# A fifth gate block pair by seven products, with the forms' sums on GpSimd

## The chip, the cores and the metric

One core of one Trainium2 chip runs the whole program. The metric is the device time of one execution in microseconds (us); the median of three runs before the change is 2079.75 us (2079.65 to 2079.78). A profile is one further execution, with its own time.

## What is computed

A trunk of two layers over 512 tokens of width 2048, in f32. Layer 0 mixes by indexed sparse attention, layer 1 by stick-breaking attention against a shared K/V. After each mixer comes the piece that the change touches:

```python
x = _layer_norm(DN_ALPHA * x + y, ln_g[i], ln_b[i])
x = x + (p[i] @ w_ple[i]) * jax.nn.sigmoid(x @ w_ple_gate[i])
```

Here `x` is 512 x 2048 and `w_ple_gate[i]` 2048 x 2048. The program keeps `x` transposed, as 16 tiles of 128 rows (features) by 512 columns (tokens).

## The kernel before

**Products in three parts.** Every f32 operand is split into a high part (fp32r) and the rest: ScalarE (ACT) makes the high part, VectorE (DVE) subtracts it (`split`, L101 to L107, for activations; `split_w`, L293 to L304, for weights, `wh` on L302 and `wl` on L303). A product is then three matmuls on TensorE (PE): high by high, high by low, low by high. In a row of the trace the operands of L121 are `wh` with `h`, of L122 `wh` with `l`, of L123 `wl` with `h`.

**Chunks.** All weight work is a list of chunks, each with a 512 KB load into one of 6 `raw` buffers, a split into one of 3 `wh`/`wl` buffers, and its matmuls. `plan` (L309) fixes once, relative to the place of a chunk in the list, when its load, its split and its additions are written; there are no costs or priorities. Each engine then takes its instructions strictly in that written order, and each waits for its own inputs and buffers; so an engine runs ahead of the place in the list as far as its inputs allow.

**A plain block pair** (`block`) makes two output tiles of 128 features in 4 chunks of 24 matmuls, 128x512 each: 96 matmuls. **A pair by seven products** (`quads`, L194) cuts the 2 x 2 block problem (two output tiles by two token halves) Strassen fashion into the products P1 to P7, each 24 matmuls of 128x256: 168 matmuls. It needs sums of weight rows (two 512 KB loads that GpSimd issues as accumulating DMAs, L286, and two DVE additions, L291) and sums of the activations, the *forms* S1 to S4.

**The gate stage of a layer** (`gate_block`) comes behind the product with `w_ple` (`ple_chunks`, which also takes part of the layer norm between its chunks). Before the change, blocks 0 to 3 (output tiles 0 to 7) are plain and pairs 4 to 7 (tiles 8 to 15) go by seven products. Blocks 0 and 1 are zipped: chunks c0 and c1 run as one over feature tiles 0 to 3, c2 and c3 over tiles 4 to 7, c4 and c5 over 8 to 11, c6 and c7 over 12 to 15. Blocks 2 and 3 are c8 to c15. While c0 to c5 run, the layer norm of the 16 tiles is finished by `ln_tiles`: for each tile DVE subtracts the mean (L944) and multiplies by the inverse deviation (L945), ACT applies gain and bias (L953; for tiles 0 and 1 it is DVE, L951) and casts the high part (L955), and DVE subtracts for the low part (L959), tile by tile, with the weights' `wl` (L303) between.

**The forms of the gate stage** are made by `g_sums(layer, j)` for feature tiles 2j and 2j+1, from the normed tiles `dT`: four additions over halves and rows of 256 columns (L783 to L786), then a split (`split`, L105 and L106). Eight such calls are hung on chunks c8 to c14, all on DVE but for the split's cast. `u_more` makes S1 and S4 during the first two seven-product pairs. Results of the `w_ple` product are kept on chip for tiles 0 to 7 and stored and loaded again for tiles 8 to 15 (`pl_store`, L989; `pl_load`, L993).

`k.tt` takes one of 78 tile buffers of 128x512; `k.soon` and `chunk.then` hang a call behind a chunk.

Of the kernel before, what the change touches and what calls it, by code (L numbers as in the profile page):

```python
# [6 lines left out]
F32 = mybir.dt.float32  # L7
F32R = mybir.dt.float32r
I32 = mybir.dt.int32
AF = mybir.ActivationFunctionType  # L10
OP = mybir.AluOpType

P = 128
T = 512
NT = T // P
D = 2048
KT = D // P
# [14 lines left out]
HALF = T // 2  # L32
# [362 lines left out]
def _emit(k, xt, pt, positions, lncols, freq, w_in, w_out, w_gate, w_ple, w_kv, w_v, w_q, out):  # L395
    nc, const = k.nc, k.const
# [185 lines left out]
    u = {}  # L582
# [181 lines left out]
    uhl, u23, u14 = {}, {}, {}  # L764
# [13 lines left out]
    def g_sums(layer, j):  # L778

        a, b = dT[2 * j], dT[2 * j + 1]  # L780
        s, t = k.tt(s="s23"), k.tt(s="s14")
        lo, hi = slice(0, HALF), slice(HALF, T)
        nc.vector.tensor_tensor(t[:, hi], b[:, hi], a[:, hi], op=OP.subtract)  # L783
        nc.vector.tensor_tensor(s[:, hi], a[:, lo], a[:, hi], op=OP.subtract)
        nc.vector.scalar_tensor_tensor(s[:, lo], t[:, hi], -1.0, a[:, lo], op0=OP.mult, op1=OP.subtract)
        nc.vector.scalar_tensor_tensor(t[:, lo], s[:, lo], -1.0, b[:, lo], op0=OP.mult, op1=OP.subtract)  # L786
        u23[j], u[2 * j + 1] = k.split(s), [t, None]
        for m in (2 * j, 2 * j + 1):
            uhl[m] = xn[m]
            if m < 8:  # L790
                dt_done(layer, m)

    once = set()

    def dt_done(layer, m):

        if (layer, m) in once:
            dT[m] = None
        once.add((layer, m))
# [13 lines left out]
    def more_forms(qs, more):  # L813
        for n, name in enumerate(("P1", "P7", "P6", "P2")):
            qs[0][name].then(lambda n=n: more("S1", (2 * n, 2 * n + 1)))
        for q, name, js in ((0, "P4", (0, 1, 2)), (0, "P5", (3, 4, 5)), (1, "P7", (6, 7))):
            qs[q][name].then(lambda js=js: more("S4", js))
# [14 lines left out]
    def u_drop(what):  # L832
        for j in range(KT // 2):
            if what == 0:
                u23.pop(j)
            else:
                uhl.pop(2 * j + (what == 1))
                if what == 2:
                    u14.pop(j)
# [65 lines left out]

    def ln_rstd():
        r, var, q = ln["rstd"], ln.pop("var"), ln.pop("q")
        nc.scalar.activation(r, var, AF.Ln)
        nc.scalar.activation(r, r, AF.Exp, scale=-0.5)
        nc.vector.tensor_tensor(q, r, r, op=OP.mult)  # L910
        nc.vector.tensor_tensor(q, q, var, op=OP.mult)
        nc.vector.tensor_scalar(q, q, -0.5, 1.5, op0=OP.mult, op1=OP.add)
        nc.vector.tensor_tensor(r, r, q, op=OP.mult)
# [29 lines left out]
    def ln_norm(m):  # L943
        nc.vector.tensor_tensor(dT[m], dT[m], ln["mean"], op=OP.subtract)  # L944
        nc.vector.tensor_tensor(dT[m], dT[m], ln["rstd"], op=OP.mult)  # L945
# [15 lines left out]
    def ln_tiles(layer, lo, hi):  # L961

        for m in range(lo, hi):
            ln_high(layer, m)
            if m + 1 < KT:
                ln_norm(m + 1)
            ln_low(m)

    def ple_done(layer, m, ps):
        t = k.tt(s="ple")  # L970
        nc.scalar.copy(t, ps)
        pl[m] = t
        if m >= 8:
            k.soon(lambda: pl_store(layer, m))
        if m == 3:
            add_squares(nc.vector)
        elif m == 5:
            ln_stats()
        elif m == 7:
            ln_rstd()  # L980
            ln_norm(0)
        elif m in (12, 14):
            ln_tiles(layer, m // 2 - 6, m // 2 - 5)
# [3 lines left out]
    def pl_store(layer, m):  # L987
        pd[m] = k.dram.tile([P, T], F32, tag=f"pl{layer}_{m}", name=k.name("pld"))
        nc.sync.dma_start(pd[m], pl.pop(m))  # L989

    def pl_load(m):
        pl[m] = k.tt(s="ple")
        nc.sync.dma_start(pl[m], pd[m])  # L993
# [55 lines left out]
    def halves(m):  # L1049
        return (slice(256, 512), slice(0, 256)) if m == KT - 1 else (slice(0, T),)  # L1050

    def gate_block(layer, fin):
        def done(b, i, ps):
            m = 2 * b + i
            sg = k.tt(s="sg")
            for c in halves(m):
                nc.scalar.activation(sg[:, c], ps[:, c], AF.Sigmoid)
                nc.vector.tensor_tensor(sg[:, c], sg[:, c], pl[m][:, c], op=OP.mult)
                nc.vector.tensor_tensor(sg[:, c], sg[:, c], dT[m][:, c], op=OP.add)
            pl[m] = None  # L1060
            dt_done(layer, m)
            fin(m, sg)

        for b in range(4):
            k.block(w_gate[layer], 4 * b, lambda m: xn[m],
                    lambda i, ps, b=b: done(b, i, ps), pops=1)
            if b == 1:
                k.zip_last()
                for ch in k.chunks[-8:]:
                    ch.mms.sort(key=lambda m: m[0])  # L1070
                k.merge_last(8)
                k.chunks[-8].after = lambda: ln_tiles(layer, 5, 8)
                for n in range(4):
                    k.chunks[n - 7].after = lambda n=n: ln_tiles(layer, 2 * n + 8, 2 * n + 10)

        for n, js in enumerate(((0,), (1,), (2,), (3,), (4,), (5,), (6, 7))):
            k.chunks[n - 8].then(lambda js=js: [g_sums(layer, j) for j in js])
        k.chunks[-1].then(xn.clear)

        def done7(n, which, t):  # L1080
            m = 2 * n + 8 + which
            for c in halves(m):
                nc.scalar.activation(t[:, c], t[:, c], AF.Sigmoid, scale=-1.0 if which else 1.0)
                nc.vector.tensor_tensor(t[:, c], t[:, c], pl[m][:, c], op=OP.mult)
                nc.vector.tensor_tensor(t[:, c], t[:, c], dT[m][:, c], op=OP.add)
            pl[m] = dT[m] = None
            fin(m, t)

        qs = k.quads([((w_gate[layer], 2 * b), (w_gate[layer], 2 * b + 1)) for b in range(4, KT // 2)], u_form, done7)
        more_forms(qs, u_more)  # L1090
        for n, q in enumerate(qs):
            q["P7"].then(lambda n=n: pl_load(2 * n + 8))
            q["P4"].then(lambda n=n: pl_load(2 * n + 9))
        last = qs[-1]
        last["P6"].then(lambda: u_drop(0))
        last["P4"].then(lambda: u_drop(1))
        last["P3"].then(lambda: u_drop(2))
        return last
# [111 lines left out]
    qs = k.quads([(where_b[a](ha), where_b[b](hb)) for a, ha, b, hb in plan_b], form, b_done)  # L1210
# [43 lines left out]
def _pairs(w, pairs):  # L1254

    v = w.reshape(4, 4, P, -1)
    v = np.stack([np.concatenate([v[..., a:a + P], v[..., b:b + P]], -1) for a, b in pairs])
    return v.transpose(0, 1, 3, 2, 4).reshape(-1, P, 1024)
# [54 lines left out]
```

## Time and profile before

| | before |
|---|---|
| median of three runs | 2079.75 us |
| profiled execution: its time | 2079.5 us |
| profiled execution: span of the core | 2077.8 us |
| TensorE busy | 2066.6 us, 99% of the span, 13600 matmuls |
| VectorE busy | 1578.0 us, 76% |
| ScalarE busy | 1078.9 us, 52% |
| GpSimd busy | 259.1 us, 12% |

Busy time is a sum over a span with very different stages. Matmuls overlap in the pipeline, so the duration of one (some 0.28 us for 256 columns) is more than the pace at which they follow each other; the pace is read from start to start. A row of the windows view gives the stretch, its length, the busy time of PE, PEld (weight loads), DVE, ACT and POOL with their instructions, the granted clock, the DMA share and GB/s. A timeline row gives start, duration, engine, line, operation and tiles; a pair of brackets at its end says how long the engine sat idle before it and for whom.

### The profile page before, as it was taken

The page shows a single profiled execution, that of the slowest core. Times are in us where ns is not written, and L with a number is a line of the kernel's source. Part 1 is how long each engine was busy: PE and PEld are TensorE (multiplying, and loading weights), DVE is VectorE, ACT ScalarE, POOL GpSimd, SP SyncE. Part 2 cuts the span into 40 slices and gives each one's busy share as a digit, 9 for nine tenths or more (in the row PEclk, how much of TensorE's full clock was granted, in tenths as well). Part 3 has the DMA queues.
Part 4 walks back from the last instruction along what each step waited for, and adds up shares of the span by engine and source line. Part 5 has one row for each costly group of instructions (what it writes and reads, how often), then busy time and mean ns, then how long its engine had stood idle before and what let it go on. Part 6 is the DMA issues. An engine that isn't in the chain of part 4 may idle for free.

```text
span 2077.8 us, 34434 instructions
## 1 busy us (share of the span) xinstructions
PE 2066.6 (99%) x13600; PEld 1900.9 (91%) x13600; DVE 1578.0 (76%) x2434; ACT 1078.9 (52%) x1749; POOL 259.1 (12%) x325
## 2 busy tenths in 40 slices
PE   9999999999999999999999999999999999999999
PEld 7987888888888998899899999999999998998898
DVE  5576976565568899787877777777777778899786
ACT  4564345455554547455555545554455554556554
POOL 5201000000000120000011111111111110121000
PEclk9999999999999999999999999999999999999999
DMA  6322322222223664457454554555555563764464
GB/s 249 102 97 76 102 92 82 70 73 71 82 88 97 189 189 148 141 163 234 132 129 130 153 162 128 134 151 151 140 149 158 136 203 112 198 178 153 132 178 127
DMA packets 89298, 284.60 MB, mean 137 GB/s; under 512 B 10160, under 2 KB 10416, under 8 KB 89136
## 3 DMA queue, kind: packets, MB, share of 16 engines
q1 hardware_dynamic: 74736, 229.97, 32.0%
q0 software_dynamic: 14400, 52.44, 14.7%
q8 instruction: 106, 1.74, 0.3%
q14 instruction: 56, 0.46, 0.1%
HBM read 266.11 MB, written 16.25 MB: 136 GB/s over the span
## 4 chain that ended last, share of the span: by engine, by line
PE 89%; DVE 4%; issue 3%; ACT 2%; DMA 1%; SPq 0%; POOL 0%; DVEq 0%; POOLq 0%; ACTq 0%
PE g L187 43%; PE g L121 13%; PE g L123 13%; PE g L122 13%; PE s L592 2%; DVE wl L303 1%; PE o L122 1%; PE o L123 1%; PE o L121 1%; PE s L121 1%; PE s L122 1%; PE s L123 1%; ACT wh L302 1%; PE s L526 1%; DMA raw<-in_w_v_dram 0%
## 5 line engine op out<-in xcount | busy, mean ns | idle before, releaser
L303 DVE TENSOR_TENSOR wl<-raw,wh 128x1024 fp32r<-128x1024 f32 (+1 forms) x513 | 631.2, 1234 | 174.7 <-ACT wh L302 172.5
L302 ACT CAST wh<-raw 128x1024 fp32r<-128x1024 f32 (+1 forms) x513 | 536.1, 1048 | 204.0 <-PE g L187 89.3
L187 PE MATMUL g<-f,wh 128*128 128x256 f32 x3360 | 619.3, 284 | 0.0
L187 PEld LDWEIGHTS g<-f,wh 128*128 128x128 f32 x3360 | 528.6, 192 | 0.8
L187 PE MATMUL g<-f,wl 128*128 128x256 f32 x1680 | 475.5, 283 | 2.3 <-DVE wl L303 2.3
L121 PE MATMUL g<-h,wh 128*128 128x512 f32 (+1 forms) x1168 | 452.4, 387 | 0.5 <-DVE o L247 0.5
L123 PE MATMUL g<-h,wl 128*128 128x512 f32 (+1 forms) x1168 | 448.4, 384 | 0.5 <-DVE wl L303 0.5
L122 PE MATMUL g<-l,wh 128*128 128x512 f32 (+1 forms) x1168 | 448.3, 384 | 0.0
L187 PEld LDWEIGHTS g<-f,wl 128*128 128x128 f32 x1680 | 322.0, 192 | 3.9 <-DVE wl L303 3.1
L187 PE MATMUL g<-h,wl 128*128 128x256 f32 x960 | 271.9, 283 | 0.2 <-DVE wl L303 0.2
L187 PE MATMUL g<-h,wh 128*128 128x256 f32 x960 | 271.7, 283 | 0.0
L187 PE MATMUL g<-l,wh 128*128 128x256 f32 x960 | 269.1, 283 | 0.0
L121 PEld LDWEIGHTS g<-h,wh 128*128 128x128 f32 x1168 | 219.3, 188 | 45.5 <-issue 3.4
L123 PEld LDWEIGHTS g<-h,wl 128*128 128x128 f32 x1168 | 219.2, 188 | 42.4 <-DVE wl L303 1.7
L122 PEld LDWEIGHTS g<-l,wh 128*128 128x128 f32 x1168 | 219.4, 188 | 40.5 <-DVE l L959 0.5
L187 PEld LDWEIGHTS g<-h,wl 128*128 128x128 f32 x960 | 184.3, 192 | 0.8 <-DVE wl L303 0.7
L187 PEld LDWEIGHTS g<-h,wh 128*128 128x128 f32 x960 | 184.3, 192 | 0.2
L187 PEld LDWEIGHTS g<-l,wh 128*128 128x128 f32 x960 | 183.1, 192 | 0.0
L291 DVE TENSOR_TENSOR raw<-raw,raw 128x1024 f32<-128x1024 f32 x100 | 121.9, 1219 | 0.2
L286 POOL DMA_DIRECT2D raw<-in_w_q_dram x60 | 53.0, 1034 | 413.5 <-issue 241.1
L650 ACT ACTIVATE pr<-pr,s 128x128 f32<-128x128 f32 (+1 forms) x64 | 36.1, 564 | 126.0 <-DVE s L649 125.7
L474 POOL TENSOR_TENSOR rb<-rb,sin 128x512 f32<-128x512 f32 (+2 forms) x29 | 35.9, 1239 | 470.3 <-ACT rb L472 292.2
(229 smaller groups left out, 2660.0 us busy)
## 6 DMA issues: line engine op xcount, KB each, us to landing
raw<-in_w_in_dram SPq DMA_DIRECT2D x97, 512.0 KB, 3.5
raw<-in_w_out_dram SPq DMA_DIRECT2D x64, 512.0 KB, 4.2
raw<-in_w_gate_dram SPq DMA_DIRECT2D x64, 512.0 KB, 3.8
raw<-in_w_q_dram SPq DMA_DIRECT2D x64, 512.0 KB, 5.0
raw<-in_w_q_dram POOLq DMA_DIRECT2D x60, 512.0 KB, 7.2
raw<-in_w_kv_dram SPq DMA_DIRECT2D x56, 512.0 KB, 4.1
raw<-in_w_out_dram POOLq DMA_DIRECT2D x24, 512.0 KB, 5.5
raw<-in_w_gate_dram POOLq DMA_DIRECT2D x16, 512.0 KB, 7.7
```

The costliest lines, as they stand in the source:

```text
L121: nc.tensor.matmul(out, ah, bh, start=start, stop=False)
L122: nc.tensor.matmul(out, ah, bl, start=False, stop=False)
L123: nc.tensor.matmul(out, al, bh, start=False, stop=stop)
L187: nc.tensor.matmul(ps[:, :HALF], a, b, start=start and j == 0 and n == 0, stop=stop and j == KT // 2 - 1 and n == 2, skip_group_check=True)
L286: self.nc.gpsimd.dma_start(ch.raw, ch.add, accum_op=OP.add)
L291: self.nc.vector.tensor_tensor(ch.raw, ch.raw, ch.plus.raw, op=OP.add)
L302: nc.scalar.copy(ch.h[:, i:i + w], ch.raw[:, i:i + w])
L303: nc.vector.tensor_tensor(ch.l[:, i:i + w], ch.raw[:, i:i + w], ch.h.bitcast(F32)[:, i:i + w], op=OP.subtract)
L474: nc.gpsimd.tensor_tensor(b[:rows, col:], b[:rows, col:], sin[:rows, col:], op=OP.mult)
L526: nc.tensor.matmul(ps[:, :n], q[rows, sl], kk[rows, :n], start=step == 0, stop=step == 2)
L592: nc.tensor.transpose(banks[b][:, off + (i - j) * P:off + (i - j + 1) * P], a["p"][i][:, j * P:(j + 1) * P], ident)
L650: nc.scalar.activation(pr[:, :n], pr[:, :n], AF.Exp, bias=mx, scale=1.0, accum_out=sm)
```

## The change

In each layer's gate stage one more pair of output tiles (6 and 7) goes by seven products: three plain blocks remain (chunks c0 to c11) and five pairs follow. The four additions of `g_sums` are written for GpSimd (`nc.gpsimd`), with signs chosen so that all four are plain two-operand additions or subtractions; S2 therefore comes out negated. The split moves into a function of its own, `g_split`, that takes the sign back: ACT casts the two halves (the second with scale -1), DVE subtracts. The sums are hung on c6 to c9, two tile pairs at a time, the splits on c8 to c11. Two more results of the `w_ple` product (tiles 6 and 7) are stored and loaded again.

```diff
     def g_sums(layer, j):
 
         a, b = dT[2 * j], dT[2 * j + 1]
-        s, t = k.tt(s="s23"), k.tt(s="s14")
+        s, t = g_made[j] = k.tt(s="s23"), k.tt(s="s14")
         lo, hi = slice(0, HALF), slice(HALF, T)
-        nc.vector.tensor_tensor(t[:, hi], b[:, hi], a[:, hi], op=OP.subtract)
-        nc.vector.tensor_tensor(s[:, hi], a[:, lo], a[:, hi], op=OP.subtract)
-        nc.vector.scalar_tensor_tensor(s[:, lo], t[:, hi], -1.0, a[:, lo], op0=OP.mult, op1=OP.subtract)
-        nc.vector.scalar_tensor_tensor(t[:, lo], s[:, lo], -1.0, b[:, lo], op0=OP.mult, op1=OP.subtract)
-        u23[j], u[2 * j + 1] = k.split(s), [t, None]
+        nc.gpsimd.tensor_tensor(t[:, hi], b[:, hi], a[:, hi], op=OP.subtract)
+        nc.gpsimd.tensor_tensor(s[:, hi], a[:, lo], a[:, hi], op=OP.subtract)
+        nc.gpsimd.tensor_tensor(s[:, lo], a[:, lo], t[:, hi], op=OP.add)
+        nc.gpsimd.tensor_tensor(t[:, lo], s[:, lo], b[:, lo], op=OP.subtract)
...
+    def g_split(j):
+
+        s, t = g_made.pop(j)
+        u23[j], u[2 * j + 1] = (k.tt(F32R, "h"), k.tt(F32R, "l")), [t, None]
+        h, l = u23[j]
+        lo, hi = slice(0, HALF), slice(HALF, T)
+        nc.scalar.copy(h[:, hi], s[:, hi])
+        nc.scalar.activation(h[:, lo], s[:, lo], AF.Identity, scale=-1.0)
+        nc.vector.tensor_tensor(l[:, hi], s[:, hi], h.bitcast(F32)[:, hi], op=OP.subtract)
+        nc.vector.scalar_tensor_tensor(l[:, lo], s[:, lo], -1.0, h.bitcast(F32)[:, lo], op0=OP.mult, op1=OP.subtract)
...
-        if m >= 8:
+        if m >= 6:
             k.soon(lambda: pl_store(layer, m))
...
-        for b in range(4):
+        for b in range(3):
             k.block(w_gate[layer], 4 * b, lambda m: xn[m],
...
-        for n, js in enumerate(((0,), (1,), (2,), (3,), (4,), (5,), (6, 7))):
-            k.chunks[n - 8].then(lambda js=js: [g_sums(layer, j) for j in js])
+        for n in range(4):
+            k.chunks[n - 6].then(lambda n=n: (g_sums(layer, 2 * n), g_sums(layer, 2 * n + 1)))
+            k.chunks[n - 4].then(lambda n=n: (g_split(2 * n), g_split(2 * n + 1)))
...
-        qs = k.quads([((w_gate[layer], 2 * b), (w_gate[layer], 2 * b + 1)) for b in range(4, KT // 2)], u_form, done7)
+        qs = k.quads([((w_gate[layer], 2 * b), (w_gate[layer], 2 * b + 1)) for b in range(3, KT // 2)], u_form, done7)
```

The order of `ln_tiles` and of the weights' splits during c0 to c5 stays as it was on DVE and on ACT. Two places show what moves; both are in layer 0, and layer 1 has the same order.

GpSimd (POOL), from the end of the layer norm's squares (`a2`) on. Before, its next instructions are the accumulating loads for the weight sums (`raw`):

```order
L892 TENSOR_TENSOR a2_1285_6509<-a2_1285_6509,sq_1409_7499 128x512
L286 DMA raw_1549_8138<-in_w_gate_dram 128x1024
L286 DMA raw_1556_8178<-in_w_gate_dram 128x1024
L286 DMA raw_1588_8349<-in_w_gate_dram 128x1024
L286 DMA raw_1611_8480<-in_w_gate_dram 128x1024
```

In the changed kernel 16 additions (four tile pairs) stand between the last square and the first accumulating load, and 16 more behind that load; the first eight, from tiles 0 to 3 (`z`):

```order
L904 TENSOR_TENSOR a2_1285_6509<-a2_1285_6509,sq_1409_7499 128x512
L783 TENSOR_TENSOR s14_1532_8051<-z_1209_5951,z_1207_5935 128x256
L784 TENSOR_TENSOR s23_1531_8050<-z_1207_5935 128x256
L785 TENSOR_TENSOR s23_1531_8050<-z_1207_5935,s14_1532_8051 128x256
L786 TENSOR_TENSOR s14_1532_8051<-s23_1531_8050,z_1209_5951 128x256
L783 TENSOR_TENSOR s14_1534_8057<-z_1218_6003,z_1217_5989 128x256
L784 TENSOR_TENSOR s23_1533_8056<-z_1217_5989 128x256
L785 TENSOR_TENSOR s23_1533_8056<-z_1217_5989,s14_1534_8057 128x256
L786 TENSOR_TENSOR s14_1534_8057<-s23_1533_8056,z_1218_6003 128x256
```

The sums that DVE made between c8 and c15 now stand on GpSimd directly behind the squares, with nothing before them in that queue but the tiles that they read.

DVE, between two weight splits behind c8. Before, the sums and the split of tile pair 0:

```order
L303 TENSOR_TENSOR wl_1536_8087<-raw_1515_7938,wh_1535_8086 128x1024
L783 TENSOR_TENSOR s14_1541_8119<-z_1209_5951,z_1207_5935 128x256
L784 TENSOR_TENSOR s23_1540_8118<-z_1207_5935 128x256
L785 SCALAR_TENSOR_TENSOR s23_1540_8118<-s14_1541_8119,z_1207_5935 128x256
L786 SCALAR_TENSOR_TENSOR s14_1541_8119<-s23_1540_8118,z_1209_5951 128x256
L106 TENSOR_TENSOR l_1543_8125<-s23_1540_8118,h_1542_8124 128x512
```

Now, the splits of tile pairs 0 and 1, which read GpSimd's sums:

```order
L303 TENSOR_TENSOR wl_1546_8115<-raw_1517_7942,wh_1545_8114 128x1024
L802 TENSOR_TENSOR l_1550_8146<-s23_1531_8050,h_1549_8145 128x256
L803 SCALAR_TENSOR_TENSOR l_1550_8146<-s23_1531_8050,h_1549_8145 128x256
L802 TENSOR_TENSOR l_1552_8152<-s23_1533_8056,h_1551_8151 128x256
L803 SCALAR_TENSOR_TENSOR l_1552_8152<-s23_1533_8056,h_1551_8151 128x256
L303 TENSOR_TENSOR wl_1560_8174<-raw_1524_7984,wh_1559_8173 128x1024
```

Per tile pair DVE keeps two instructions of 256 columns out of four of 256 and one of 512.

## Rows read from the trace of the kernel before

**Rows 1.** The page, busy time and the chain that ended last

```profile
PE 2066.6 (99%) x13600; PEld 1900.9 (91%) x13600; DVE 1578.0 (76%) x2434; ACT 1078.9 (52%) x1749; POOL 259.1 (12%) x325
...
PE 89%; DVE 4%; issue 3%; ACT 2%; DMA 1%; SPq 0%; POOL 0%; DVEq 0%; POOLq 0%; ACTq 0%
```

**Rows 2.** Windows of 5 us in layer 1's gate stage

```profile
1904.00:1909.00 5.00, 5.00 (x24) 4.14 (x23) 4.93 (x10) 3.49 (x6) 0.00 (x0) 1.00 0.79 284
...
1919.00:1924.00 5.00, 5.00 (x23) 3.97 (x22) 4.93 (x8) 3.68 (x6) 0.00 (x0) 1.00 0.30 104
...
1964.00:1969.00 5.00, 5.00 (x24) 4.14 (x23) 1.99 (x3) 1.65 (x2) 0.00 (x0) 1.00 0.01 2
```

**Rows 3.** Timeline of PE, plain blocks of layer 1's gate stage

```profile
1905.12 0.39 PE L123 MATMUL g<-h,wl 128*128 128x512 f32 x1
...
1919.40 0.39 PE L123 MATMUL g<-h,wl 128*128 128x512 f32 x1
...
1919.86 0.50 PE L122 MATMUL g<-l,wh 128*128 128x512 f32 x1
```

**Rows 4.** Chain that ended last, layer 1's pairs by seven products: start, us, what

```profile
1992.01 80.64 PE g L187 x672
```

**Rows 5.** Timeline of DVE, both gate stages: layer norm, weight splits, sums

```profile
825.19 0.69 DVE L959 TENSOR_TENSOR l<-o,h 128x512 fp32r<-128x512 f32 x1
...
1904.58 0.54 DVE L951 TENSOR_SCALAR z<-z,lncol 128x512 f32<-128x512 f32 x1
...
1917.80 0.68 DVE L944 TENSOR_TENSOR o<-o,mean 128x512 f32<-128x512 f32 x1
1918.52 0.69 DVE L945 TENSOR_TENSOR o<-o,rstd 128x512 f32<-128x512 f32 x1
1919.12 0.68 DVE L959 TENSOR_TENSOR l<-o,h 128x512 fp32r<-128x512 f32 x1
1919.77 1.23 DVE L303 TENSOR_TENSOR wl<-raw,wh 128x1024 fp32r<-128x1024 f32 x1
...
1924.81 1.23 DVE L303 TENSOR_TENSOR wl<-raw,wh 128x1024 fp32r<-128x1024 f32 x1
...
1934.90 1.23 DVE L303 TENSOR_TENSOR wl<-raw,wh 128x1024 fp32r<-128x1024 f32 x1
...
1952.28 0.42 DVE L783 TENSOR_TENSOR s<-z,z 128x256 f32<-128x256 f32 x1
```

**Rows 6.** Timeline of POOL: two-operand additions and products, and an accumulating load

```profile
118.66 1.01 POOL L474 TENSOR_TENSOR rb<-rb,sin 128x384 f32<-128x384 f32 x1 [17.87 <-ACT rb L472]
...
305.98 1.29 POOL L474 TENSOR_TENSOR rb<-rb,sin 128x512 f32<-128x512 f32 x1 [25.29 <-ACT rb L472]
...
769.87 1.30 POOL L892 TENSOR_TENSOR a<-a,sq 128x512 f32<-128x512 f32 x1 [1.56 <-ACT sq L890]
...
776.06 1.46 POOL L892 TENSOR_TENSOR a<-a,sq 128x512 f32<-128x512 f32 x1 [4.90 <-ACT sq L890]
...
1883.53 2.06 POOL L892 TENSOR_TENSOR a<-a,sq 128x512 f32<-128x512 f32 x1 [0.16 <-ACT sq L890]
1957.47 0.88 POOL L286 DMA_DIRECT2D raw<-in_w_gate_dram  x1 [71.88 <-DVE s L785]
```

**Rows 7.** Timeline of DVE beside the POOL rows at 769.87 and 776.06

```profile
769.32 0.68 DVE L891 TENSOR_TENSOR a<-a,o 128x512 f32<-128x512 f32 x1
769.92 1.79 DVE L878 TENSOR_TENSOR o<-o,lnc 128x512 f32<-128x512 f32 x1
...
775.15 1.22 DVE L303 TENSOR_TENSOR wl<-raw,wh 128x1024 fp32r<-128x1024 f32 x1 [0.57 <-ACT wh L302]
776.29 1.78 DVE L891 TENSOR_TENSOR a<-a,o 128x512 f32<-128x512 f32 x1
```

**Rows 8.** Timeline of ACT, gain and bias of feature tile 7 in layer 1

```profile
1917.32 0.82 ACT L953 ACTIVATE o<-o,lncol 128x512 f32<-128x512 f32 x1 [0.46 <-DVE o L945]
```

**Rows 9.** Timeline of SP's queue: the load behind which the first addition waits

```profile
1952.39 0.34 SPq L207 DMA_DIRECT2D raw<-in_w_gate_dram  x1
```

More of the change, by code (lines that the diff above doesn't have):

```diff
@@ L780, in g_sums @@
         a, b = dT[2 * j], dT[2 * j + 1]
-        s, t = k.tt(s="s23"), k.tt(s="s14")
+        s, t = g_made[j] = k.tt(s="s23"), k.tt(s="s14")
         lo, hi = slice(0, HALF), slice(HALF, T)
-        nc.vector.tensor_tensor(t[:, hi], b[:, hi], a[:, hi], op=OP.subtract)
-        nc.vector.tensor_tensor(s[:, hi], a[:, lo], a[:, hi], op=OP.subtract)
-        nc.vector.scalar_tensor_tensor(s[:, lo], t[:, hi], -1.0, a[:, lo], op0=OP.mult, op1=OP.subtract)
-        nc.vector.scalar_tensor_tensor(t[:, lo], s[:, lo], -1.0, b[:, lo], op0=OP.mult, op1=OP.subtract)
-        u23[j], u[2 * j + 1] = k.split(s), [t, None]
+        nc.gpsimd.tensor_tensor(t[:, hi], b[:, hi], a[:, hi], op=OP.subtract)
+        nc.gpsimd.tensor_tensor(s[:, hi], a[:, lo], a[:, hi], op=OP.subtract)
+        nc.gpsimd.tensor_tensor(s[:, lo], a[:, lo], t[:, hi], op=OP.add)
+        nc.gpsimd.tensor_tensor(t[:, lo], s[:, lo], b[:, lo], op=OP.subtract)
         for m in (2 * j, 2 * j + 1):
             uhl[m] = xn[m]
-            if m < 8:
+            if m < 6:
                 dt_done(layer, m)
+    g_made = {}
+    def g_split(j):
[7 more added lines that the diff above has]
+        nc.vector.scalar_tensor_tensor(l[:, lo], s[:, lo], -1.0, h.bitcast(F32)[:, lo], op0=OP.mult, op1=OP.subtract)
     once = set()
@@ L1074, in gate_block @@
                     k.chunks[n - 7].after = lambda n=n: ln_tiles(layer, 2 * n + 8, 2 * n + 10)
-        for n, js in enumerate(((0,), (1,), (2,), (3,), (4,), (5,), (6, 7))):
-            k.chunks[n - 8].then(lambda js=js: [g_sums(layer, j) for j in js])
+        for n in range(4):
+            k.chunks[n - 6].then(lambda n=n: (g_sums(layer, 2 * n), g_sums(layer, 2 * n + 1)))
+            k.chunks[n - 4].then(lambda n=n: (g_split(2 * n), g_split(2 * n + 1)))
         k.chunks[-1].then(xn.clear)
         def done7(n, which, t):
-            m = 2 * n + 8 + which
+            m = 2 * n + 6 + which
             for c in halves(m):
@@ L1087, in done7 @@
             fin(m, t)
-        qs = k.quads([((w_gate[layer], 2 * b), (w_gate[layer], 2 * b + 1)) for b in range(4, KT // 2)], u_form, done7)
+        qs = k.quads([((w_gate[layer], 2 * b), (w_gate[layer], 2 * b + 1)) for b in range(3, KT // 2)], u_form, done7)
         more_forms(qs, u_more)
         for n, q in enumerate(qs):
-            q["P7"].then(lambda n=n: pl_load(2 * n + 8))
-            q["P4"].then(lambda n=n: pl_load(2 * n + 9))
+            q["P7"].then(lambda n=n: pl_load(2 * n + 6))
+            q["P4"].then(lambda n=n: pl_load(2 * n + 7))
         last = qs[-1]
@@ L1295 @@
         w_out=np.stack([_out(np.asarray(w)[0], blocks) for w in (w_out_a, w_out_b)]),
-        w_gate=np.stack([_out(w, blocks, 4) for w in np.asarray(w_ple_gate)]),
+        w_gate=np.stack([_out(w, blocks, 3) for w in np.asarray(w_ple_gate)]),
         w_ple=np.stack([_natural(w, D) for w in np.asarray(w_ple)]),
```

## The prediction

> **What bounds the kernel now.** I read the page first: PE is busy for 99% of the span and holds 89% of the chain that ended last [rows 1]. So only two things can move the time: the matmul time itself, and a wait that gets into PE's way. Next I read the gate stage by windows, because a share over the whole span hides stages. Two limits stand side by side there: while the layer norm is finished (up to 1939 us) DVE is busy for 4.93 of each 5 us beside a full PE, and by 1964 it is down to 1.99 [rows 2]. The reader is to see that DVE is nearly critical in the first part and has room in the second. The granted clock is 1.00, the 2.4 GHz level, in all three. Third, the timelines of PE and DVE in the first part, to see how much DVE may be late. The low part of feature tile 7 ends at 1919.12 + 0.68 = 1919.80, and the matmul that reads it, at 1919.86, takes 0.50 where its neighbours take 0.39 [rows 3, 5]: DVE has no slack there at all. Layer 0 has the same row at 825.19 [rows 5].
>
> **The matmuls, a gain.** Plain blocks: from 1905.12 to 1919.40 there are 63 matmuls of 512 columns, 14.28 / 63 = 0.2267 us each [rows 3]; a block pair has 96, 21.76 us. Seven products: 672 matmuls of 256 columns in 80.64 us, 0.1200 each and without a gap [rows 4]; a pair has 168, 20.16 us. Swapping one for the other gives 1.60 us a layer, 3.2 us in all, 0.15% of the time. That is under 0.2% (some 4 us), about the least that a measurement of this kernel can tell from no change. PE has no other gap in this stage that could close.
>
> **The sums on GpSimd, a loss.** The code hangs the sums on c6 to c9, but that only orders them. GpSimd's queue holds nothing between the last square of the layer norm and the sums; before, it slept 71.88 us there [rows 6]. So each group of four starts as soon as its two tiles are normed. Tile 1 is ready at 1904.58 + 0.54 = 1905.1 [rows 5], tile 7 at 1917.32 + 0.82 = 1918.1 [rows 8], tiles 3 and 5 between them. The 16 additions of the first four pairs thus fall into the stretch in which DVE is full.
>
> What happens when both engines add is in the trace. A 512-column addition on POOL starts at 769.87; the DVE addition issued at 769.92 ends only at 771.71, 1.79 us instead of the 0.68 of its predecessor [rows 6, 7]. POOL ends at 771.17, so DVE's 0.54 of work came wholly behind it: a loss of 1.10 us. The other pair shows who wins: at 776.06 POOL is issued while DVE runs a weight split (775.15 to 776.37); POOL gets in right behind it (it ends at 777.52), and the DVE instruction already in the queue takes 1.78 [rows 6, 7]. So every POOL addition gets in behind at most one DVE instruction and stops the next.
>
> Price of one with 256 columns: POOL takes 1.29 for 512 and 1.01 for 384 [rows 6], so 0.73 for 256. DVE lost 1.10 of 1.30, 0.2 less than POOL's whole time; 0.73 - 0.2 = 0.53, and half of 1.10 gives 0.55. I take 0.53, as some DVE instructions start 0.12 late anyway (L945 starts 0.72 behind L944, L959 0.60 behind L945 [rows 5]). The smallest price is nothing; the largest is the whole 0.73.
>
> How late DVE gets: three pairs (12) are past before tile 7 is normed; then the additions of the fourth stop L945 of tile 8 and L959 of tile 7, so tile 7's low part is 14 x 0.53 = 7.4 us late, with no slack. The weight split behind it (1919.77, needed some 0.5 after its end) is 15 x 0.53 = 8.0 late, and the next one (1924.81 to 1926.04) is 16 x 0.53 = 8.5 late with about 1.0 of slack, as chunk c4 starts at 1926.5 (48 matmuls behind the start of c2, whose 20th is the one at 1919.86) and reads `wl` with its third matmul. All three say the same: PE ends this stretch **7.5 us late**, in each layer.
>
> **The rest.** The second group of 16 stands on POOL behind the first accumulating load, which waits for a load issued (1952.39) when c10's split is through, 5.1 us before the addition's issue (1957.47) [rows 6, 9]. With four chunks fewer that split is c6's (1934.90 to 1936.13 [rows 5]), now 8.5 late: the addition comes at about 1949.7, is issued in 0.88, and the 16 sums follow. Each waits for a DVE instruction (0.6) at worst: 16 x (0.73 + 0.6) = 21 us, to 1972. The last splits are wanted when the pairs start, 21.76 earlier than before plus 7.5, at 1992.01 - 21.76 + 7.5 = 1977.8. That holds with 6 us to spare, and the 8.5 that DVE loses here falls into a stretch with room [rows 2]; I take nothing, and up to 2 us a layer for the range. Taken off DVE: four instructions of 0.42 and one of 0.69 per pair become two of 0.42, some 12 us a layer, but where PE did not wait for it: no gain. ACT casts two halves instead of a whole, some 0.1 more for each of eight pairs, beside 1.65 busy of 5 [rows 2]. The two more stores and loads on SP's queue are 256 KB each, and the two more accumulating loads take 0.88 each on POOL's [rows 6]; four such pairs already run without a gap [rows 4], so the fifth costs nothing. The sign of S2 costs nothing: it rides on the cast and the subtraction. If any of this cover goes, PE waits at the first P7.
>
> **Sum.** Per layer 7.5 - 1.6 = 5.9; twice that is 11.8. The profiled execution took 2079.5, so 2091.3; the median stands 0.25 above it: **2091.6 us**, slower by 0.57%.
>
> **Where a rule weighs in.** The rows show 1.10 us lost to a 1.30 us instruction [rows 6, 7]. The Trainium skill, SBUF — State Buffer, section Who interferes with whom, says that a VectorE instruction with two SBUF inputs and a GpSimd instruction that reads SBUF take the same port pair, and that whoever issues first holds it for the whole instruction while the other fully blocks. By it each sum would cost 0.73 and the time would be that of the second rival below; the trace agrees that one blocks, with 0.2 less than the whole.
>
> **Rivals.**
> 1. *The sums cost PE nothing* (not slower). If POOL gave way to DVE, or the sums ran only where they are written (behind c6, at 1943 and later), DVE would stay on time up to 1939 and only the matmul gain is left: 2079.75 - 3.2 = **2076.5**. It decides at tile 7's low part: at under 1.6 us of lateness there the change still gains. For it: DVE has room behind 1939. Against: both pairs of rows, in which POOL gets in first, and its empty queue. Chance 12%.
> 2. *POOL holds DVE for its whole time.* 16 x 0.73 = 11.7 us late, less 1.0 at c4: 10.7; per layer 9.1, twice 18.2: **2098**. For it: the price per instruction may have a fixed part. Against: 1.79 - 0.68. Chance 14%.
> 3. *The second 16 come late as well.* The longest row of such an addition with waits is 2.06 [rows 6]; at that pace they end 33 us behind 1950.6, at 1983.6, and PE waits some 6 us at the first P7 besides: 2 x 6 more, **2103**. Against: that row is for 512 columns. Chance 7%.
>
> **How the numbers follow.** My own case has 64%, with 2086 to 2096 by its bounds (prices from 0.35, two thirds of what I take, to 0.60, and up to 1 us a layer at the start of the pairs). 3% is left for a gain over 0.2%, for which I see no mechanism: the matmuls give 3.2 us at most. The range takes my case and most of the second rival and leaves out the first and the third: 2085 to 2100. Slower by over 0.2%: 64 + 14 + 7 = 85%. Within 0.2%: rival 1, 12%. Faster: 3%.
>
> **What would show it.** Right, if in the changed profile POOL's rows of L783 to L786 start near 1905 in layer 1's gate stage (and 811 in layer 0's), last 0.7 to 1.3 us, and DVE's L956, L957 and L971 beside them take about 1.2 instead of 0.69; if PE sits idle for about 7 us in pieces between tile 4 and c4 of each gate stage, named as waiting for DVE's L971 and L303; and if the five pairs run without a gap, 100.8 us for 840 matmuls. Wrong, if DVE's rows there keep their 0.69, if POOL's sums start behind c6, or if PE's idle time lies at the first P7 instead.

## The result and the profile after

The changed kernel takes **2090.61 us** (median of six runs, 2089.22 to 2091.22) against 2079.76 us of before in the same session: 10.85 us more, ratio 1.0051 with a 95% interval of 1.0039 to 1.0063. The prediction was 2091.6 us. The profiled execution has a span of 2089.0 us, 11.2 more than before.

The page of the changed kernel, busy time and the chain that ended last (before: [rows 1]):

```profile
PE 2071.6 (99%) x13744; PEld 1906.6 (91%) x13744; DVE 1597.3 (76%) x2402; ACT 1087.7 (52%) x1779; POOL 334.3 (16%) x393
...
PE 88%; DVE 5%; issue 3%; ACT 2%; DMA 1%; POOL 0%; SPq 0%; POOLq 0%; DVEq 0%; ACTq 0%
```

DVE has 32 instructions fewer than before and is busy for 19 us more. That is the first sign: its instructions have become longer. PE's share is unchanged, so the page alone does not show where 11 us went; the stage does.

Timeline of POOL in the changed kernel, layer 1's gate stage:

```profile
1910.33 1.11 POOL L783 TENSOR_TENSOR s<-z,z 128x256 f32<-128x256 f32 x1 [19.61 <-DVE z L963]
1911.40 1.18 POOL L784 TENSOR_TENSOR s<-z 128x256 f32<-128x256 f32 x1
...
1932.38 1.60 POOL L786 TENSOR_TENSOR s<-s,o 128x256 f32<-128x256 f32 x1
1953.12 0.89 POOL L286 DMA_DIRECT2D raw<-in_w_gate_dram  x1 [19.14 <-DVE l L971]
...
1971.45 0.81 POOL L786 TENSOR_TENSOR s<-s,o 128x256 f32<-128x256 f32 x1
```

The first sum starts when tile 1 is normed, as the bracket says, not behind c6. The first 16 sums fill 1910 to 1934, the stretch of the layer norm; the second 16 follow the accumulating load.

Timeline of DVE beside them (before: [rows 5], 0.68 and 0.69 each):

```profile
1909.10 0.68 DVE L971 TENSOR_TENSOR l<-z,h 128x512 fp32r<-128x512 f32 x1
...
1910.88 1.11 DVE L957 TENSOR_TENSOR z<-z,rstd 128x512 f32<-128x512 f32 x1
1911.91 1.23 DVE L971 TENSOR_TENSOR l<-z,h 128x512 fp32r<-128x512 f32 x1
1913.06 1.22 DVE L956 TENSOR_TENSOR z<-z,mean 128x512 f32<-128x512 f32 x1
1914.32 1.11 DVE L957 TENSOR_TENSOR z<-z,rstd 128x512 f32<-128x512 f32 x1
...
1930.51 1.22 DVE L971 TENSOR_TENSOR l<-o,h 128x512 fp32r<-128x512 f32 x1
1931.65 1.75 DVE L303 TENSOR_TENSOR wl<-raw,wh 128x1024 fp32r<-128x1024 f32 x1
```

Four sums, four long rows: 0.42, 0.55, 0.54 and 0.42 more than their own time. Up to tile 7's low part (1930.51 + 1.22 = 1931.73) there are 14 such rows with 6.85 us of excess, 0.49 for a sum. Layer 1 starts 5.12 us later than before (its first L971 at 1909.10, the same instruction at 1903.98 before), so this low part, which ended at 1919.80 [rows 5], is 1931.73 - 1924.92 = 6.8 us late.

PE in the same stretch, by its timeline and by windows (columns as in [rows 2]; the clock is the third number from the right):

```profile
1923.01 0.49 PE L123 MATMUL g<-h,wl 128*128 128x512 f32 x1 [0.63 <-DVE wl L303]
...
1926.43 0.50 PE L122 MATMUL g<-l,wh 128*128 128x512 f32 x1 [2.00 <-DVE l L971]
...
1928.89 0.80 PE L122 MATMUL g<-l,wh 128*128 128x512 f32 x1 [0.54 <-DVE l L971]
...
1931.78 0.79 PE L122 MATMUL g<-l,wh 128*128 128x512 f32 x1
...
1934.08 0.58 PE L121 MATMUL g<-h,wh 128*128 128x512 f32 x1
```

```profile
1919.00:1924.00 5.00, 4.37 (x18) 3.20 (x18) 4.97 (x5) 2.67 (x4) 3.44 (x4) 1.00 0.02 4
1924.00:1929.00 5.00, 2.46 (x9) 1.16 (x7) 4.93 (x7) 2.16 (x3) 2.89 (x3) 0.86 0.31 101
1929.00:1934.00 5.00, 5.00 (x11) 3.55 (x12) 4.96 (x5) 3.02 (x5) 4.74 (x4) 0.50 0.00 0
1934.00:1939.00 5.00, 5.00 (x22) 4.07 (x21) 4.93 (x8) 3.65 (x5) 0.00 (x0) 0.95 0.29 105
```

PE waits for DVE's L971 and L303, as forecast, but the idle times in these brackets come to 3.2 us only (3.5 with one of 0.29 at 1913.19). The third window shows where a part of the rest stands: PE is "busy" for 5.00 of 5 us with 11 matmuls instead of some 22, because the granted clock is 0.50 there, the 1.2 GHz level. A busy share alone would hide that.

The chain in the five pairs of layer 1 (before: [rows 4]):

```profile
1983.42 100.80 PE g L187 x840
```

840 matmuls at 0.1200 without a gap, so nothing is lost there. From the first low part of layer 1 to the first of these matmuls it is 74.15 us (1909.10 to 1983.25). Before, that low part is this row:

```profile
1903.98 0.68 DVE L959 TENSOR_TENSOR l<-z,h 128x512 fp32r<-128x512 f32 x1
```

From it to the first matmul of the pairs, at 1991.85, it is 87.87 us; less one plain pair (21.76), 66.11. So PE is 8.04 us late in layer 1, and by the same reckoning 7.1 in layer 0 (810.13 to 883.32; before, 810.03 to 897.92, less 21.76). Less 1.60 for the matmuls in each, that is 11.9. The span grew by 11.2: outside the gate stages the trace of the changed kernel is 0.7 shorter, in a wait of PE for a `wl` between the two stages (0.4) and behind the last matmul of the pairs (0.35). Neither was in the forecast, and their cause stays open.

### The profile page after: what moved, and what is told of

Same layout as the page of the kernel before. It is cut to its first block, busy times and chain, and to the rows that moved or that the text cites. A ratio compares the mean times of both kernels' runs of the same rounds, so it can differ in the third digit from the quotient of the medians.

```text
span 2089.0 us, 34855 instructions
## 1 busy us (share of the span) xinstructions
PE 2071.6 (99%) x13744; PEld 1906.6 (91%) x13744; DVE 1597.3 (76%) x2402; ACT 1087.7 (52%) x1779; POOL 334.3 (16%) x393
## 4 chain that ended last, share of the span: by engine, by line
PE 88%; DVE 5%; issue 3%; ACT 2%; DMA 1%; POOL 0%; SPq 0%; POOLq 0%; DVEq 0%; ACTq 0%
PE g L187 44%; PE g L121 12%; PE g L122 12%; PE g L123 12%; PE s L592 2%; DVE wl L303 1%; PE o L122 1%; PE o L123 1%; PE o L121 1%; PE s L121 1%; PE s L122 1%; PE s L123 1%; PE s L526 1%; ACT wh L302 1%; DVE l L971 1%
## 5 line engine op out<-in xcount | busy, mean ns | idle before, releaser
L303 DVE TENSOR_TENSOR wl<-raw,wh 128x1024 fp32r<-128x1024 f32 (+1 forms) x519 | 642.4, 1241 | 171.8 <-ACT wh L302 169.8
L122 PE MATMUL g<-l,wh 128*128 128x512 f32 (+1 forms) x1104 | 426.4, 386 | 5.9 <-DVE l L971 5.9
L121 PE MATMUL g<-h,wh 128*128 128x512 f32 (+1 forms) x1104 | 429.2, 389 | 0.5 <-DVE o L247 0.5
L123 PE MATMUL g<-h,wl 128*128 128x512 f32 (+1 forms) x1104 | 425.5, 385 | 1.8 <-DVE wl L303 1.8
L187 PE MATMUL g<-h,wl 128*128 128x256 f32 x1056 | 299.0, 283 | 0.2 <-DVE wl L303 0.2
L187 PE MATMUL g<-h,wh 128*128 128x256 f32 x1056 | 298.8, 283 | 0.0
L187 PE MATMUL g<-l,wh 128*128 128x256 f32 x1056 | 295.9, 283 | 0.0
L122 PEld LDWEIGHTS g<-l,wh 128*128 128x128 f32 x1104 | 208.2, 189 | 49.3 <-DVE l L971 11.8
L121 PEld LDWEIGHTS g<-h,wh 128*128 128x128 f32 x1104 | 208.2, 189 | 43.2 <-issue 3.4
L123 PEld LDWEIGHTS g<-h,wl 128*128 128x128 f32 x1104 | 208.1, 188 | 42.1 <-DVE wl L303 4.1
L187 PEld LDWEIGHTS g<-h,wl 128*128 128x128 f32 x1056 | 202.7, 192 | 0.8 <-DVE wl L303 0.6
L187 PEld LDWEIGHTS g<-h,wh 128*128 128x128 f32 x1056 | 202.7, 192 | 0.2
L187 PEld LDWEIGHTS g<-l,wh 128*128 128x128 f32 x1056 | 201.4, 192 | 0.0
```

The costliest lines, as they stand in the source:

```text
L121: nc.tensor.matmul(out, ah, bh, start=start, stop=False)
L122: nc.tensor.matmul(out, ah, bl, start=False, stop=False)
L123: nc.tensor.matmul(out, al, bh, start=False, stop=stop)
L187: nc.tensor.matmul(ps[:, :HALF], a, b, start=start and j == 0 and n == 0, stop=stop and j == KT // 2 - 1 and n == 2, skip_group_check=True)
L303: nc.vector.tensor_tensor(ch.l[:, i:i + w], ch.raw[:, i:i + w], ch.h.bitcast(F32)[:, i:i + w], op=OP.subtract)
```

## The experiments

All ratios are to runs of the kernel before on the same chip. "Over before" is the difference of the medians.

| run | us | over before | ratio, 95% interval |
|---|---|---|---|
| sums on DVE, behind c6 to c9 | 2079.89 | +0.3 | 1.0002 (0.9993 to 1.0010) |
| GpSimd's sums, four pairs | 2093.14 | +13.5 | 1.0066 (1.0053 to 1.0079) |
| sums on DVE, 16 idle additions on GpSimd | 2092.82 | +13.2 | 1.0064 (1.0050 to 1.0077) |
| GpSimd for two tile pairs only | 2083.48 | +3.9 | 1.0019 (1.0010 to 1.0027) |
| sums on DVE, one chunk earlier | 2077.31 | -2.6 | 0.9987 (0.9978 to 0.9996) |
| GpSimd's sums held back | 2091.79 | +11.9 | 1.0056 (1.0043 to 1.0070) |
| 16 idle copies | 2083.82 | +4.0 | 1.0019 (1.0010 to 1.0028) |
| 16 idle memsets | 2079.75 | -0.1 | 0.9999 (0.9990 to 1.0008) |
| TensorE's waits filled | 2089.91 | +10.1 | 1.0049 (1.0032 to 1.0065) |
| 8 idle additions of 512 columns | 2096.95 | +17.2 | 1.0083 (1.0068 to 1.0098) |

### The sums back on DVE

```diff
-        nc.gpsimd.tensor_tensor(t[:, hi], b[:, hi], a[:, hi], op=OP.subtract)
+        nc.vector.tensor_tensor(t[:, hi], b[:, hi], a[:, hi], op=OP.subtract)
...
-        nc.gpsimd.tensor_tensor(t[:, lo], s[:, lo], b[:, lo], op=OP.subtract)
+        nc.vector.tensor_tensor(t[:, lo], s[:, lo], b[:, lo], op=OP.subtract)
```

> The changed kernel with one thing put back: the 32 sums of each layer's gate stage are made by VectorE again, at the same place in the program (behind c6 to c9); five pairs by seven products stay. Theory (GpSimd's sums stop VectorE while the layer norm is finished): VectorE's rows of the layer norm are 0.69 us again, tile 7's low part is on time, TensorE does not wait, and only the matmul gain of 1.60 us a layer is left: 2076.5 us (2075.5 to 2078). Rival (the loss comes from the fifth pair itself: its two more stores and loads, its additions of weight rows, or the sums being made four chunks earlier): the time stays near 2090, and TensorE's idle time lies behind c6 or at the first P7.

Measured: 2079.89 us, the time of before. Neither number came. The 10.6 us between this kernel and the changed one, each against its own before, hang on the engine of the sums alone, which is the theory; but the time is 3.4 above the theory's, so the whole gain of the fifth pair is missing. DVE's timeline in this run shows what a sum costs there, and PE's where the gain went:

```profile
1947.33 0.42 DVE L783 TENSOR_TENSOR s<-z,z 128x256 f32<-128x256 f32 x1
1947.66 0.42 DVE L784 TENSOR_TENSOR s<-z 128x256 f32<-128x256 f32 x1
...
1948.79 0.42 DVE L783 TENSOR_TENSOR s<-z,z 128x256 f32<-128x256 f32 x1
```

```profile
1975.80 0.39 PE L187 MATMUL g<-l,wh 128*128 128x256 f32 x1
...
1976.47 0.39 PE L187 MATMUL g<-l,wh 128*128 128x256 f32 x1
...
1977.94 0.39 PE L187 MATMUL g<-h,wl 128*128 128x256 f32 x1 [0.97 <-DVE wl L303]
```

Four sums take DVE 1.46 us, 0.365 each. With one plain block less, DVE has less time for the same work: from 1944.66 to 1984.98 it has one pause, of 0.50 us, and PE waits at the first pair for the forms' last low parts and for a `wl`, together 2.0 us (from the first matmul of the pairs at 1970.37 to their end it is 102.99 us instead of 100.96), more than the 1.60 that the fifth pair gains.

### GpSimd's sums without the fifth pair

```diff
-        for b in range(3):
+        for b in range(4):
             k.block(w_gate[layer], 4 * b, lambda m: xn[m],
...
-        qs = k.quads([((w_gate[layer], 2 * b), (w_gate[layer], 2 * b + 1)) for b in range(3, KT // 2)], u_form, done7)
+        qs = k.quads([((w_gate[layer], 2 * b), (w_gate[layer], 2 * b + 1)) for b in range(4, KT // 2)], u_form, done7)
```

The numbers of the output tiles that go with it (stores, loads, the weights' layout) are those of before.

> The other half of the change alone: the sums on GpSimd with the new split, at the same distance ahead of the pairs, but four plain blocks and four pairs by seven products, as before. Theory: the matmul gain is missing and the loss is that of the changed kernel, 10.85 + 2 x 1.60 = 14.05 us over before: 2093.8 us (2092.5 to 2095). Rival (the fifth pair makes the loss): 2079.8 us, no change. If the second 16 sums were a part of the loss, they have 21.8 us more time here, and the time is below 2092.

Measured: 2093.14 us. The move of the sums makes the whole loss, also where the pairs start 21.8 us later, so the second 16 sums have no part in it. The changed kernel is 2.7 us better than this one, relative to their own before: the fifth pair's gain, 3.2 forecast.

### The disputed cost by itself

16 additions per layer on GpSimd that nobody reads, while DVE makes the sums:

```diff
+        if j < 4:
+            e = k.tt(s="idle")
+            for c, d in ((hi, a), (lo, a), (hi, b), (lo, b)):
+                nc.gpsimd.tensor_tensor(e[:, c], b[:, c], d[:, lo], op=OP.add)
```

> The kernel with the sums back on VectorE, and beside them 16 additions of 256 columns per layer on GpSimd that nobody reads, each behind the normed tiles of the pairs 0 to 3 as the real sums were: the disputed cost by itself, without anything that waits for GpSimd's results. Theory (an addition on GpSimd that reads two operands stops VectorE's own for some 0.49 us): tile 7's low part is 14 x 0.49 = 6.8 us late and the time is that of the kernel with the sums on VectorE plus about 14 us, 2090.5 us (2088.5 to 2092.5). Rival (the loss came from waiting for GpSimd's results, or from the splits): as the kernel with the sums on VectorE, 2076.5 us.

Measured: 2092.82 us, 12.9 more than without them: 6.5 a layer, 0.46 for each of the 14 ahead of tile 7. That is 0.3 above the range, which was reckoned from 2076.5 for the kernel without them. Nobody waits for GpSimd's results here, so it is not a wait for the sums: it is DVE that is stopped.

### Half of them

```diff
+        eng = nc.gpsimd if j < 2 else nc.vector
```

(and the four additions on `eng`).

> The changed kernel with GpSimd making the sums of the pairs 0 and 1 alone (8 additions per layer in the stretch where the layer norm is finished); VectorE makes those of the pairs 2 to 7 behind c7 to c9. Theory (the loss is proportional to the additions that fall ahead of tile 7): 8 x 0.49 = 3.9 us late per layer instead of 6.8, less the 1.60 of the matmuls: 2079.75 + 2 x 2.3 = 2084.4 us (2083 to 2086). Rival (VectorE has some slack that swallows the first few, so that only the later ones count): below 2081. Rival (any use of GpSimd here costs the whole): 2090.

Measured: 2083.48 us; 3.88 / 2 + 1.60 = 3.5 us late per layer, 0.44 for a sum; DVE has eight longer rows per layer, with 3.88 us of excess, 0.49 each. The loss goes with the number of sums, without slack ahead of the first.

### What of a GpSimd instruction stops DVE

The 16 idle additions replaced by 16 copies of 256 columns:

```diff
-            for c, d in ((hi, a), (lo, a), (hi, b), (lo, b)):
-                nc.gpsimd.tensor_tensor(e[:, c], b[:, c], d[:, lo], op=OP.add)
+            for c, d in ((hi, a), (lo, a), (hi, b), (lo, b)):
+                nc.gpsimd.tensor_copy(e[:, c], b[:, c])
```

> As the run with 16 additions on GpSimd that nobody reads, but with 16 copies of 256 columns in their place: one operand read instead of two, at the same place behind the same tiles. Theory A (only an instruction of two operands stops VectorE's): as the kernel with the sums on VectorE, 2079.9 us (2079 to 2081), VectorE's rows 0.69. Theory B (any GpSimd instruction that reads on-chip memory stops VectorE's additions, as the Trainium skill says in SBUF — State Buffer, section Who interferes with whom): between 2086 and 2093, as with the additions, in proportion to how long a copy takes.

or by 16 memsets:

```diff
+            nc.gpsimd.tensor_copy(e[:, :1], b[:, :1])
+            for c in (hi, lo, hi, lo):
+                nc.gpsimd.memset(e[:, c], 0.0)
```

> The same with 16 memsets of 256 columns per layer, each four behind a copy of one column that holds them back until the tiles are normed: GpSimd writes as much and reads next to nothing. Theory A and B (what stops VectorE is reading): 2079.9 us (2079 to 2081), with at most four stops of some 0.2 us for the one-column copies. Rival (a busy GpSimd stops VectorE whatever it does, or the waits and signals between the two do): 2085 to 2093.

or by eight additions of 512 columns:

```diff
+            nc.gpsimd.tensor_tensor(e, b, a, op=OP.add)
+            nc.gpsimd.tensor_tensor(e, b, a, op=OP.subtract)
```

> The kernel with the sums on VectorE and eight additions of 512 columns per layer on GpSimd that nobody reads, two behind each of the tile pairs 0 to 3: as many columns as the run with 16 of 256, in half as many instructions. Theory A (a GpSimd addition stops VectorE for its length less 0.2 us): 1.30 - 0.2 = 1.10 each, as in the rows of before; 7 of the 8 ahead of tile 7's low part, 7.7 us per layer: 2079.9 + 15.4 = 2095.3 us (2094 to 2097). Theory B (the price goes by columns, 0.465 per 256 as measured with 16 additions): 7 x 0.93 = 6.5 per layer: 2092.9 us (2092 to 2094). Theory C (the price is that of an instruction, whatever its width): 7 x 0.465 = 3.3 per layer: 2086.4 us.

Measured: 2083.82, 2079.75 and 2096.95 us. POOL and DVE with the copies (four in the first row):

```profile
1907.39 3.20 POOL L786 COPY idle<-z 128x256 f32<-128x256 f32 x4 [19.57 <-DVE z L967]
```

```profile
1907.96 0.77 DVE L961 TENSOR_TENSOR z<-z,rstd 128x512 f32<-128x512 f32 x1
1908.65 0.88 DVE L975 TENSOR_TENSOR l<-z,h 128x512 fp32r<-128x512 f32 x1
```

With the memsets:

```profile
1906.31 1.06 POOL L787 MEMSET idle<- 128x256 f32 x4
```

```profile
1906.36 0.69 DVE L962 TENSOR_TENSOR z<-z,rstd 128x512 f32<-128x512 f32 x1
1906.97 0.68 DVE L976 TENSOR_TENSOR l<-z,h 128x512 fp32r<-128x512 f32 x1
```

With the wide additions:

```profile
1912.95 1.67 POOL L785 TENSOR_TENSOR idle<-z,z 128x512 f32<-128x512 f32 x1 [19.59 <-DVE z L967]
```

```profile
1913.51 1.67 DVE L961 TENSOR_TENSOR z<-z,rstd 128x512 f32<-128x512 f32 x1
1915.10 1.76 DVE L975 TENSOR_TENSOR l<-z,h 128x512 fp32r<-128x512 f32 x1
```

A memset stops nothing: DVE keeps its 0.69, and the time is that of before. A copy stops DVE for 0.08 to 0.20 us, so both theories missed: it does stop it, at under a third of an addition's price. An addition of 512 columns stops it for 0.95 to 1.10, 1.03 in the mean. The idle additions of 256 took 0.46. Both are the length of an undisturbed one (1.30 [rows 6] and 0.73) less 0.27, so theory A has the form right and its 0.2 is a little small; all eight fall ahead of tile 7's low part and not seven. With eight, theory B (0.93 each) gives 2094.8 us, 2.2 below the measured time. Why a copy, which also reads, stops so much less is not shown. The Trainium skill, SBUF — State Buffer, section Who interferes with whom, says that a VectorE instruction with two SBUF inputs contends with a GpSimd instruction that reads SBUF and not with one that only writes; the copies and memsets agree. The Trainium skill gives the loss there as the whole instruction of the other engine; here it is 0.42 to 0.55 of the 0.73 that an undisturbed sum takes.

### The sums held back behind the layer norm

```diff
+        if j == 0:
+            nc.gpsimd.tensor_copy(t[:, :1], xn[15][1].bitcast(F32)[:, :1])
         nc.gpsimd.tensor_tensor(t[:, hi], b[:, hi], a[:, hi], op=OP.subtract)
```

> The changed kernel with one instruction more per layer on GpSimd, ahead of the first sum: a copy of one column of the low part of tile 15, so that no sum starts before the layer norm is finished. Theory (the loss comes from where the sums fall in time): the stretch up to 1939 is as before, without waits. A sum on GpSimd takes 0.49 us from VectorE where VectorE itself makes one in 0.365, so the 32 sums, now all behind 1939, load VectorE about 2 to 4 us more than when it makes them itself (which is late by 1.7 at the first pair): 3 to 5 us late at the first P7 and P6, less 1.60: 2083.5 us (2080 to 2087). Rival (what counts is that GpSimd makes them, wherever): 2090. Rival (GpSimd's sums fill VectorE's idle time and cost nothing there): 2076.5.

Measured: 2091.79 us, above the range and nearer to the first rival's 2090. But the rows put the loss at the pairs and not into the layer norm: the mechanism was the theory's, its size was not. POOL's timeline, PE's waits and the windows of this run:

```profile
1946.72 0.74 POOL L785 TENSOR_TENSOR s<-z,z 128x256 f32<-128x256 f32 x1
1947.42 1.72 POOL L786 TENSOR_TENSOR s<-z 128x256 f32<-128x256 f32 x1
...
1981.92 1.61 POOL L788 TENSOR_TENSOR s<-s,o 128x256 f32<-128x256 f32 x1
```

```profile
1981.31 0.38 PE L187 MATMUL g<-h,wl 128*128 128x256 f32 x1 [1.23 <-DVE wl L303]
1986.52 0.58 PE L187 MATMUL g<-l,wh 128*128 128x256 f32 x1 [2.67 <-DVE l L804]
1988.66 0.58 PE L187 MATMUL g<-h,wl 128*128 128x256 f32 x1 [0.67 <-DVE wl L303]
```

```profile
1984.00:1989.00 5.00, 1.81 (x6) 1.52 (x7) 4.93 (x11) 2.87 (x8) 1.25 (x2) 0.74 0.83 171
1989.00:1994.00 5.00, 5.00 (x28) 5.00 (x28) 4.44 (x6) 1.36 (x3) 0.00 (x0) 0.58 1.01 285
```

The stretch up to 1939 is undisturbed: the first product starts on time, 66.12 us behind layer 1's first low part (66.11 before). But the 32 sums end at 1983.5, 6.6 us after that start at 1976.93, since an addition here waits for a DVE instruction and then lasts up to 1.72 instead of 0.74. PE waits for the last low parts, and the granted clock is 0.74 and 0.58 behind these waits. Held back in this way the sums cost about as much as ahead of it; other places behind the layer norm were not tried.

### TensorE's waits filled

Ten matmuls that nobody reads in the changed kernel, eight ahead of tile 5's low part and two ahead of tile 6's:

```diff
         nc.tensor.matmul(out, ah, bh, start=start, stop=False)
+        if fill:
+            f = self.ps("s")
+            for _ in range(fill):
+                nc.tensor.matmul(f, ah, bh, start=True, stop=True)
...
+                k.chunks[-6].fill = {2: 8, 4: 2}
```

> The changed kernel with ten matmuls of 512 columns more per layer on TensorE, whose results nobody reads: eight where it waits 2.0 us for the low part of tile 5, two where it waits 0.5 us for that of tile 6. They take 10 x 0.2267 = 2.3 us of time in which TensorE stands idle anyway, so they should delay nothing. Theory (the granted clock fell at 1927.7 in layer 1 and at 828.5 in layer 0 because TensorE had stood idle): the clock stays at 1.00 through both stretches; in layer 1 the six matmuls behind tile 7's low part at half the pace (1931.78 to 1934.08) come at 0.23 us again, 1.3 us less; in layer 0 TensorE waits for VectorE at tile 7 in any case, nothing less: 2089.3 us (2088 to 2090.5), and the rest of the loss, VectorE's lateness of 6.7 us per layer, stays. Rival (the clock fell for something else): the windows show 0.5 to 0.9 again at the same places, and 2090.6 us.

Measured: 2089.91 us. The two kernels' own medians don't tell 0.7 us apart, but the rows do. PE's timeline and windows, where the changed kernel had a clock of 0.86 and 0.50:

```profile
1925.19 1.98 PE L125 MATMUL s<-h,wh 128*128 128x512 f32 x8
1927.36 0.50 PE L126 MATMUL g<-l,wh 128*128 128x512 f32 x1 [0.19 <-DVE l L975]
...
1932.71 0.50 PE L126 MATMUL g<-l,wh 128*128 128x512 f32 x1 [1.22 <-DVE l L975]
```

```profile
1924.00:1929.00 5.00, 4.81 (x20) 3.66 (x21) 4.93 (x5) 1.44 (x2) 3.82 (x4) 1.00 0.32 105
1929.00:1934.00 5.00, 3.42 (x15) 2.16 (x14) 4.96 (x6) 3.75 (x5) 3.81 (x4) 1.00 0.00 0
```

The clock stays at 1.00, so its fall came of TensorE's standing idle. From layer 1's first low part to the pairs it is 73.19 us instead of 74.15: 1.0 us of the loss in layer 1 was the clock. In layer 0 it is 73.2 in both, so there the clock cost nothing (1099.0 us from its first low part to layer 1's in both), and with the clock kept PE is 7.1 late in either layer. The profiled spans are the same, 2089.0, because layer 0's stage starts 0.9 later in this run; the gain is read from the stage and not from the time. At tile 7, where the slow matmuls had hidden it, PE now shows the wait for DVE: 1.22 us. The rest is DVE's lateness.

### A version that beats both

The sums stay on DVE, five pairs stay, and sums and splits are written one chunk earlier, from the first run above:

```diff
-            k.chunks[n - 6].then(lambda n=n: (g_sums(layer, 2 * n), g_sums(layer, 2 * n + 1)))
-            k.chunks[n - 4].then(lambda n=n: (g_split(2 * n), g_split(2 * n + 1)))
+            k.chunks[n - 7].then(lambda n=n: (g_sums(layer, 2 * n), g_sums(layer, 2 * n + 1)))
+            k.chunks[n - 5].then(lambda n=n: (g_split(2 * n), g_split(2 * n + 1)))
```

> The kernel with five pairs and all sums on VectorE, with the sums and their splits written one chunk earlier (sums behind c5 to c8, splits behind c7 to c10). Why: with the sums behind c6 to c9 VectorE is busy without a break from 1944.7 to 1985 in layer 1 and late for the first pair's P7 and P6 (TensorE's rows at 1975.80, 1976.47 and 1977.94), by about the 1.6 us that the fifth pair gains, while it idles for some 3.3 us around 1939 to 1944.7. Theory (only VectorE's order is at fault): eight sums (8 x 0.365 = 2.9 us) move into that idle time, the wait at the first pair is gone, and the matmul gain is left: 2076.5 us (2075.5 to 2077.5). Rival (the fifth pair costs something else, its stores, loads or added weight rows, besides that wait): 2079 to 2080, or a wait at another place.

Measured: 2077.31 us, faster than before (the interval excludes 1) and 13.4 us under the changed kernel, each against its own before. DVE's timeline, and the chain in the pairs:

```profile
1940.18 0.42 DVE L783 TENSOR_TENSOR s<-z,z 128x256 f32<-128x256 f32 x1
...
1942.76 0.43 DVE L786 TENSOR_TENSOR s<-s,z 128x256 f32<-128x256 f32 x1
```

```profile
1969.91 100.80 PE g L187 x840
```

Eight sums stand where DVE had been idle, and the pairs run without a gap. Of the 3.2 us that the two swaps are worth, 2.6 came. One new wait per layer for a `wl` behind the early sums (a bracket of 0.27 at 1959.17 in layer 1, 0.5 from start to start) is of the size of the rest.

## Why the prediction was right

**What bounds, right.** PE's time and waits for DVE ahead of tile 7. All the loss lies there; the pairs have no gap, the second 16 sums end at 1972.3, which is 1967.1 on before's scale (by 1972 forecast).

**Where the sums run, right.** They started at tile 1, not at c6. In the layer norm their rows last 0.87 to 1.60, somewhat more than the 0.7 to 1.3 expected.

**The price, a little high.** 0.53 forecast, 0.49 in the rows, 0.44 to 0.46 by the times of the runs with half and with idle additions. Tile 7's low part was 6.8 us late instead of 7.4; the number of sums ahead of it, 14, was right. The second rival (0.73 each, 2098) is out.

**PE's lateness, right in sum and not in make-up.** 7.5 per layer forecast; 7.1 and 8.04 measured, 7.6 in the mean. Two errors offset each other: the price was 0.6 us a layer too high, and the fall of the clock, which no step had, added 1.0 in layer 1. So it is partly luck that the sum came this close. "Idle for about 7 us in pieces" was therefore wrong as a sign: the bracketed waits are 3 to 4 us. Part of the lost time stands as slow matmuls, and a bracket starts at a matmul's modelled end, 0.39 to 0.50 behind its start, where the next could have followed after 0.23.

**"Taken off DVE, no gain", half right.** PE did not wait for those sums before. But with a plain block less it would have, as the run with the sums on DVE shows (2.0 us a layer). I had not priced that the swap itself shortens DVE's time.

**The first rival's second condition, wrong.** I gave 2076.5 us if the sums ran only behind c6. Held back behind the layer norm they cost 11.9 us, by the third rival's mechanism: late for the first pair. What does give about that time is the sums on DVE, one chunk earlier.

## What to carry to other kernels

Work moved from a busy DVE to GpSimd was no relief where both read two tiles from on-chip memory: each GpSimd addition took 0.44 to 0.49 us from a DVE that makes the same one in 0.365. Before moving work off an engine, look for its idle time a few places earlier in its own order; 2.9 us of it was enough here. And a GpSimd instruction runs when its inputs and its queue allow, not where it is written, so ask what runs on DVE at that time.

## What the runs showed that I had not expected

In layer 1 a stall was paid for a second time, by TensorE's clock: after PE had been idle for 0.6 and 2.0 us within 4 us, the granted clock went from 1.00 to 0.50, the 1.2 GHz level, at 1927.7, stayed there through the wait of 0.5 us and came back at 1934.1; matmuls in the waits of 2.0 and 0.5 us kept it at 1.00 and gave 1.0 us back. In layer 0 the same fall cost nothing, because PE met DVE's next late result in any case. How much idle time is needed for it was not tried: the run with eight sums had waits of 0.6, 0.5, 0.3 and 0.3 us and kept 1.00 in these windows:

```profile
1919.00:1924.00 5.00, 3.59 (x13) 2.21 (x13) 4.93 (x8) 2.87 (x5) 0.00 (x0) 1.00 0.31 105
1924.00:1929.00 5.00, 4.72 (x21) 3.52 (x20) 4.93 (x8) 3.69 (x6) 0.00 (x0) 1.00 0.22 75
```
